# A planner that keeps TensorE's excursions to small products apart, in a GLA + RWKV-7 macaron block

## The chip, the cores and the metric

The kernel runs on one core of a Trainium2 chip. The metric is device time in microseconds of one execution. One execution in the hardware profiler gives the trace that is read here.

## The reference, cut to what matters

One layer on a sequence of 1024 rows of width 1024, all in float32:

```
x = x + 0.5 * swiglu(rms_norm(x), ffn1)          # d_ff = 2816
p = rms_norm(x) @ w_in                           # 3344 columns
o = [ GLA mixer(p) , RWKV-7 mixer(p) ]           # 512 + 512 columns, both recurrent in time
x = x + o @ w_out
x = x + 0.5 * swiglu(rms_norm(x), ffn2)
return rms_norm(x)
```

The GLA mixer keeps a 64 x 128 state for each of 4 heads. The RWKV-7 mixer keeps a 64 x 64 state for each of 8 heads; a state is multiplied by a decay, takes a rank-one correction from itself and a rank-one input at every row. Both are computed by chunks of rows, so that most of the work is small matrix products, and the chunks of one head follow one another.

## The kernel before, in words

**Halves.** The sequence is cut into two halves of 512 rows, A and B. Weights and activations of the large products are each split into a high part and a rest of type fp32r, and one large product is three matmuls (high x high, high x rest, rest x high), each 128 x 128 by 128 x 512. In this text these are the *plain products*. The mixers' products are plain float32 with tiles of 32 to 128 rows and columns: the *small products*.

**Order of the stages.** FFN 1 of A; the joint part of FFN 1 for both halves (a Strassen-like scheme, `joint_up` and `joint_down`); then for A: norm, projections (`proj`), mixers, output projection (`outproj`); then the same for B. While the mixers of A run, the ten remaining hidden blocks of B's FFN 1 are computed (generator `f1b`), and while the mixers of B run those of A's FFN 2 (`f2a`). The end is the joint part of FFN 2 and the final norm.

**The mixers (`mixers`, line 1226).** The mixers of a half are four generators, "streams", which issue a step's instructions and then yield a latency in ns or a tag to wait for:

- `loop`: RWKV's recurrence, four units u of two chunks each. A chunk has three steps: `pz`, then `pu`, then `px` and `py` together. Each needs what VectorE (DVE) or ScalarE (ACT) made of the one before.
- `prep`: for each unit, `pg` (Gram matrices), an inversion of 16 x 16 blocks in 15 rounds on VectorE (lines 106 to 108, no TensorE work) up to a transposition (line 115), then `p1`, `p1b`, `p2`, `p2b`, `pav`. Unit u may start when `loop` is through with unit u-2.
- `norm`: for each unit after `loop` is through with it, a group norm on VectorE and ScalarE (lines 226 to 233), transposes `pyT`, eight ScalarE instructions (line 244), two additions and a store.
- `both_gl`: the GLA mixer for two pairs of heads: `pkv`, `pA`, five times `pB`, `po`, two times `pt`.

**The planner** (lines 1265 to 1283) writes TensorE's order out by hand (`manual_schedule` for that engine). It keeps a clock of its own, `T.ns`, which each matmul moves on by a cost (class `PE`, line 34; 216.3 ns for a plain product). A step that was made sets its stream's due time to `T.ns` plus the latency times `SLACK` (1.49). When a stream is due, every free stream due within `NEAR` (254 ns) makes one step; then as many plain products follow as the excursion's time times `FILL` (0.3) holds, at least one; when none is due, one plain product. An *excursion* is a run of small products between plain ones. The plain products come from the filler (`f1b` or `f2a`), one matmul at each call, and end at the marker `AFTER` (hidden block 8 of 10, line 364): 480 in a half. From then on `filling` is false, and steps are written down when they come due, with nothing between.

What the planner does not fix is left to the framework, which orders the other engines, and TensorE outside of the planned part, by priority and by its own estimate of readiness. So the 96 plain products that come next in the program (`pdn` of blocks 6 and 7, then `pgu` of block 9) are laid between the last planned steps. After the last `pyT` come its ScalarE and VectorE work, a store to DRAM, the loads of the mixed rows (`outprep`, line 1285) and the output projection's first product (`pout`).

Of the kernel before, what the change touches and what calls it, by code (L numbers as in the profile page):

```python
# [372 lines left out]
BUFS = dict(s2=7, W=4, WA=2, WN=4, AR=2, UV=2, AV=2, R64=2, s1=2, i2=3, g1=3, s3=2)  # L373
SLACK = 1.490
FILL = 0.3
PAHEAD = 2
NEAR = 254.150
NH, NL, NR = 6, 6, 4
# [14 lines left out]
def block_kernel(tc, ctx, x, consts, coff, vecs, finaln, wgu, wdn, win_t, win_v, w_out, alw, wa2, g2, out):  # L393
    nc = tc.nc
    V, S, T, GP = nc.vector, nc.scalar, PE(nc.tensor), nc.gpsimd
# [67 lines left out]
    def mm3(ps, l, r, start, stop):  # L463
        T.matmul(ps, l[0], r[0], start=start, stop=False)
        T.matmul(ps, l[0], r[1], start=False, stop=False)
        T.matmul(ps, l[1], r[0], start=False, stop=stop)
# [231 lines left out]
    def stage_f(f):  # L698

        H = wk.tile([P, VW], F32R, tag="wH", bufs=NH, name="wH")[:, :HT]  # L700
        L = wk.tile([P, VW], F32R, tag="wL", bufs=NL, name="wL")[:, :HT]
        halved(f, H, L)
        return H, L
# [51 lines left out]
    def hid_dram(w, j, op):  # L755
        return dram(f"hid{w}_{j}_{op}", [P, 2 * HT])
# [92 lines left out]
    def joint_down(w, c1, c2, ep, hold, between, first=None, early=False):  # L849


        d1, d2 = slice(0, HT), slice(HT, D)
        n = len(PAIRS)
        kept = {}

        def right(i, j):

            if j not in kept:
                t = hold(j)
                for k, f in enumerate(PAIRS[j]):  # L860
                    nc.sync.dma_start(t[:, 2 * k:2 * k + 2].rearrange("p c d->p (c d)"), wdn[w][P * f:P * f + P, :])
                kept[j] = [t[:, k] for k in range(4)]
            lo0, hi0, lo1, hi1 = kept[j]
            if i in (1, 2, 3):
                return stage_f({1: lo0, 2: lo1, 3: hi1}[i])
            t = EG[:, 4 + next(turn) % 3]
            if i == 5:
                GP.tensor_tensor(t, hi0, lo0, op=SUB)
            else:
                GP.tensor_tensor(t, hi1, hi0, op=SUB)  # L870
                if i != 7:
                    GP.tensor_tensor(t, t, lo0, op=ADD)
                if i == 4:
                    GP.tensor_tensor(t, t, lo1, op=SUB)
            return stage_f(t)

        def banks(k):
            return [(pa if 4 * k + t < 5 else pm).tile([P, HT], F32, tag="pa" if 4 * k + t < 5 else "pm", name="pjd") for t in range(4)]

        def sums():  # L880
            return ep.tile([P, 7, HT], F32, tag="EG", name="EG")

        turn = iter(range(1000))
        EG = sums() if early else None
        for i in ORDER:
            ps = banks(int(i in (6, 7, 4)))
            for j in range(n):
                u = right(i, j)
                hh = first(j) if first and i == 1 else ep.tile([P, 2, HT], F32R, tag="hh", bufs=6, name="hh")
                nc.sync.dma_start(hh.bitcast(F32).rearrange("p a t->p (a t)"), hid_dram(w, j, i))  # L890
                for t in range(4):
                    to = slice(P * t, P * t + P)
                    mm3(ps[t], (hh[:, 0, to], hh[:, 1, to]), u, j == 0, j == n - 1)
            EG = EG or sums()
            E = [EG[:, t] for t in range(4)]
            for t in range(4):
                def add(x, v, k=0.5):
                    V.scalar_tensor_tensor(x, v, k, x, op0=MULT, op1=ADD)  # L898

                if i > 1:  # L900
                    x1 = c1.x[t]
                if i not in (1, 6):
                    x2 = c2.x[t]
                if i == 1:
                    S.copy(E[t], ps[t])
                    if t == 3:
                        between[1](E[t][:, 0:1])
                elif i == 6:
                    add(x1[:, d1], E[t])
                    V.tensor_tensor(E[t], ps[t], E[t], op=ADD)  # L910
                    if t == 3:
                        between[6](E[t][:, 0:1])
                elif i == 2:
                    add(x1[:, d1], ps[t])
                    add(x1[:, d2], E[t])
                elif i == 7:
                    V.tensor_tensor(E[t], ps[t], E[t], op=ADD)
                    if t == 3:
                        for y, e in zip(c2.x, E):
                            add(y[:, d1], e)  # L920
                            add(y[:, d2], e)
                        if i in between:
                            between[i](E[t][:, 0:1])
                elif i == 5:
                    add(x2[:, d2], ps[t])
                    add(x1[:, d2], ps[t])
                    if t == 3 and i in between:
                        between[i](x1[:, 0:1])
                elif i == 4:
                    add(x2[:, d1], ps[t], -0.5)  # L930
                else:
                    add(x1[:, d2], ps[t])
# [16 lines left out]
    def proj(h):  # L949
# [19 lines left out]
        def weights(ti):  # L969
            return [stage(win_t[2 * ti + kh]) for kh in range(2)]  # L970

        def product(nm):
            ps = pm.tile([P, HT], F32, tag="pm", name="pp")
            ti = TTILES.index(nm)
            us = staged.pop(ti, None) or weights(ti)
            for i in range(ti + 1, min(ti + 1 + PAHEAD, len(TTILES))):
                if ti > 1 and i not in staged:
# [248 lines left out]
    def mixers(h, filler, last):  # L1226
        hf = h.i
        d = lambda nm, cols=HT: dram(f"{nm}_{hf}", [P, cols])

        def wide(nm, cols=HT):  # L1230
            return dram(f"{nm}_{hf}", [P, 4 * cols]).rearrange("p (q t)->p q t", q=4)

        quad = Quad(g, {n: wide(n) for n in ("bv", "g", "vt", "wn0", "wn1", "mix")} |
                    {"BK": wide("BK", 2 * HT), "AR": wide("AR", 2 * HT).rearrange("p q (x t)->p q x t", x=2)})

        def gl(p):
            return gla_unit(g, p, {n: d(f"{'la' if n == 'cum' else 'kk' if n == 'k' else n}{p}") for n in ("q", "k", "cum", "qx", "kN")},
                            dram(f"vn_{hf}", [HT, HT])[:, 256 * p:256 * p + 256],
                            [d(f"go{2 * p + j}") for j in range(2)], [d(f"mix{2 * p + j}") for j in range(2)])

        tags = set()

        class Stream:
            def __init__(self, gen):
                self.gen, self.at, self.wait, self.done = gen, T.ns, None, False

            def step(self):
                try:
                    lat = next(self.gen)
                    while isinstance(lat, str) and lat[0] != "?":  # L1250
                        tags.add(lat)
                        lat = next(self.gen)
                    self.wait, lat = (lat[1:], 0.0) if isinstance(lat, str) else (None, lat)
                    self.at = T.ns + lat * SLACK
                except StopIteration:
                    self.done = True

            def free(self):
                return self.wait is None or self.wait in tags

        def both_gl():
            for p in range(2):
                yield from gl(p)

        todo = [Stream(x) for x in (quad.loop(), quad.prep(), quad.norm(), both_gl())]
        filling = True
        with tc.manual_schedule(engines={mybir.EngineType.PE}):
            while True:
                todo = [s for s in todo if not s.done]
                if not todo:  # L1270
                    break
                can = [s for s in todo if s.free()]
                t0, n = T.ns, 1
                if any(s.at <= t0 for s in can):
                    for s in can:
                        if s.at <= T.ns + NEAR:
                            s.step()
                    n = int((T.ns - t0) * FILL / 216.0 + 0.999)
                for _ in range(n):
                    if filling and next(filler, last) == last:  # L1280
                        filling = False
                if not filling and not any(s.at <= T.ns for s in can):
                    T.ns = min(s.at for s in can)
# [119 lines left out]
    def first(j):  # L1403
        if j < 4 and j % 2 == 0:
            front[j] = B.pool.tile([P, 4, HT], F32R, tag=XN[j // 2], name="hhf")
        return front[j // 2 * 2][:, 2 * (j % 2):2 * (j % 2) + 2] if j < 4 else ep.tile([P, 2, HT], F32R, tag="hh", bufs=6, name="hh")
# [147 lines left out]
```

## Time and profile before

| | us |
|---|---|
| median of 3 runs | 2138.57 |
| lowest, highest | 2127.97, 2830.62 |
| the profiled execution, its own time | 2131.11 |
| its span in the trace | 2129.3 |

The span reaches from the first to the last instruction; the other 1.8 us of that execution lie around it. The profiled execution is 0.35% below the median. The run of 2830.62 us stands apart from the two others. The trace gives each instruction's start, duration, engine, source line and tiles, who released it where it waited, and the granted clock of TensorE as a share of 2.4 GHz.

### The profile page before, as it was taken

The page shows a single profiled execution, that of the slowest core. Times are in us where ns is not written, and L with a number is a line of the kernel's source. Part 1 is how long each engine was busy: PE and PEld are TensorE (multiplying, and loading weights), DVE is VectorE, ACT ScalarE, POOL GpSimd, SP SyncE. Part 2 cuts the span into 40 slices and gives each one's busy share as a digit, 9 for nine tenths or more (in the row PEclk, how much of TensorE's full clock was granted, in tenths as well). Part 3 has the DMA queues.
Part 4 walks back from the last instruction along what each step waited for, and adds up shares of the span by engine and source line. Part 5 has one row for each costly group of instructions (what it writes and reads, how often), then busy time and mean ns, then how long its engine had stood idle before and what let it go on. Part 6 is the DMA issues. An engine that isn't in the chain of part 4 may idle for free.

```text
span 2129.3 us, 36214 instructions
## 1 busy us (share of the span) xinstructions
PE 2044.5 (96%) x13516; PEld 1633.4 (77%) x13516; DVE 1454.7 (68%) x3043; ACT 909.3 (43%) x1699; POOL 551.4 (26%) x558
## 2 busy tenths in 40 slices
PE   8999999989999999999999999999998999998998
PEld 7777888868788877767878887777776788886886
DVE  6675788747738867765476957866587577864675
ACT  6432333422446644543375644633343243432143
POOL 0411446475211300000001220000221245647610
PEclk9999999999999999999999999999998999999999
DMA  5433344587446764323435583432633334449652
GB/s 194 128 115 105 128 149 158 189 322 277 141 144 215 232 203 137 107 89 121 145 129 187 193 263 105 145 100 85 208 129 109 109 120 157 156 160 350 235 171 74
DMA packets 172639, 345.20 MB, mean 162 GB/s; under 512 B 17296, under 2 KB 56240, under 8 KB 172464
## 3 DMA queue, kind: packets, MB, share of 16 engines
q1 hardware_dynamic: 145312, 251.13, 36.1%
q0 software_dynamic: 23552, 80.76, 10.4%
q10 hardware_dynamic: 3600, 11.01, 1.5%
q8 instruction: 106, 1.74, 0.3%
q14 instruction: 69, 0.57, 0.1%
HBM read 243.21 MB, written 99.61 MB: 161 GB/s over the span
## 4 chain that ended last, share of the span: by engine, by line
PE 81%; DVE 7%; DMA 6%; ACT 3%; issue 2%; POOL 1%; SPq 0%; ACTq 0%; DVEq 0%
PE pju L43 21%; PE pgu L43 16%; PE pp L43 12%; PE pdn L43 10%; PE pjd L43 6%; PE pout L43 4%; PE pv L43 2%; PE py L43 2%; DMA hh<-d_hid 1%; PE po L43 1%; DVE x L898 1%; DVE wL L460 1%; DVE T L696 1%; DMA xw<-d_xf 1%; PE pt L46 1%
## 5 line engine op out<-in xcount | busy, mean ns | idle before, releaser
L460 DVE TENSOR_TENSOR wL<-raw,wH 128x512 fp32r<-128x512 f32 (+1 forms) x382 | 273.4, 724 | 259.9 <-ACT wH L459 259.4
L459 ACT CAST wH<-raw 128x512 fp32r<-128x512 f32 (+1 forms) x382 | 234.1, 618 | 392.6 <-PE pgu L43 126.1
L43 PE MATMUL pgu<-xnH,wH 128*128 128x512 f32 (+1 forms) x656 | 259.1, 396 | 0.3 <-ACT xnH L518 0.2
L43 PE MATMUL pgu<-xnH,wL 128*128 128x512 f32 (+1 forms) x656 | 257.9, 394 | 0.2 <-DVE wL L460 0.2
L43 PE MATMUL pgu<-xnL,wH 128*128 128x512 f32 (+1 forms) x656 | 257.8, 394 | 0.2 <-DVE xnL L519 0.2
L43 PE MATMUL pju<-T,wH 128*128 128x512 f32 x768 | 240.7, 394 | 2.4 <-ACT wH L695 2.4
L43 PE MATMUL pjd<-wH,hh 128*128 128x512 f32 x640 | 208.9, 407 | 15.0 <-DMA hh<-d_hid 14.5
L43 PEld LDWEIGHTS pju<-T,wH 128*128 128x128 f32 x768 | 144.3, 188 | 36.7 <-ACT wH L695 3.3
L43 PEld LDWEIGHTS pjd<-wH,hh 128*128 128x128 f32 x640 | 125.0, 195 | 47.3 <-issue 16.8
L43 PE MATMUL pju<-T,wL 128*128 128x512 f32 x384 | 151.4, 394 | 0.0
L43 PEld LDWEIGHTS pgu<-xnH,wH 128*128 128x128 f32 x656 | 123.8, 189 | 28.0 <-ACT xnH L518 1.0
L43 PEld LDWEIGHTS pgu<-xnH,wL 128*128 128x128 f32 x656 | 123.7, 189 | 27.9 <-issue 0.7
L43 PEld LDWEIGHTS pgu<-xnL,wH 128*128 128x128 f32 x656 | 123.8, 189 | 27.1 <-DVE xnL L519 1.0
L43 PE MATMUL pdn<-wH,hH 128*128 128x512 f32 x320 | 132.2, 414 | 11.3 <-DVE hf L668 7.7
L43 PE MATMUL pp<-xnH,wH 128*128 128x512 f32 x352 | 140.7, 400 | 0.0
L43 PE MATMUL pp<-xnL,wH 128*128 128x512 f32 x352 | 138.9, 395 | 0.0
L43 PE MATMUL pp<-xnH,wL 128*128 128x512 f32 x352 | 138.9, 395 | 0.0
L43 PE MATMUL pjd<-wL,hh 128*128 128x512 f32 x320 | 130.3, 407 | 5.8 <-DVE wL L696 5.8
L43 PE MATMUL pdn<-wH,hL 128*128 128x512 f32 x320 | 131.5, 411 | 1.2 <-DVE hL L672 1.2
L43 PE MATMUL pdn<-wL,hH 128*128 128x512 f32 x320 | 130.4, 408 | 0.9 <-DVE wL L460 0.9
L631 DVE SCALAR_TENSOR_TENSOR x<-pdn,x 128x512 f32<-128x512 f32 x144 | 98.7, 687 | 33.0 <-PE pdn L43 31.8
L696 DVE TENSOR_TENSOR wL<-s,wH 128x512 fp32r<-128x512 f32 x96 | 99.1, 1034 | 29.7 <-ACT wH L695 29.6
(393 smaller groups left out, 4317.5 us busy)
## 6 DMA issues: line engine op xcount, KB each, us to landing
raw<-in_wgu_dram SPq DMA_DIRECT2D x256, 256.0 KB, 2.7
hh<-d_hid SPq DMA_DIRECT2D x80, 512.0 KB, 4.4
d_hid<-hh POOLq DMA_DIRECT2D x76, 512.0 KB, 3.7
raw<-in_win_t_dram SPq DMA_DIRECT2D x88, 256.0 KB, 3.2
raw<-in_wdn_dram SPq DMA_DIRECT2D x80, 256.0 KB, 2.7
wdk<-in_wdn_dram SPq DMA_DIRECT2D x24, 512.0 KB, 7.0
d_x<-x SPq DMA_DIRECT2D x20, 512.0 KB, 2.6
raw<-in_w_out_dram SPq DMA_DIRECT2D x32, 256.0 KB, 3.0
```

The costliest lines, as they stand in the source:

```text
L43: return self.t.matmul(out,lhsT,rhs,**kw)
L46: return self.t.transpose(out,in_,idn)
L459: S.copy(H, raw)
L460: V.tensor_tensor(L, raw, H.bitcast(F32), op=SUB)
L631: V.scalar_tensor_tensor(h.x[tt][:, co], ps, 0.5, h.x[tt][:, co], op0=MULT, op1=ADD)
L696: V.tensor_tensor(L, f, H.bitcast(F32), op=SUB)
L898: V.scalar_tensor_tensor(x, v, k, x, op0=MULT, op1=ADD)
```

## The change: what it does

A constant `APART` of 1700 ns is added, and the planner notes in `back` its clock at the end of the last excursion that had TensorE work. While the filler lasts, no stream makes a step before the planner's clock is at `back + APART`, even if it is due. A plain product counts 216.3 ns, so eight of them lie between two excursions (seven count 1514 ns). Streams that fall due in the meantime make their steps together afterwards. Steps without TensorE work are held back too, but do not set `back`. The first edit of the diff, in `joint_down`, drops a Python name that is not read in that pass and issues nothing.

```diff
 FILL = 0.3
+APART = 1700.0
...
-                if i not in (1, 6):
+                if i not in (1, 2, 6):
                     x2 = c2.x[t]
...
         filling = True
+        back = 0.0
...
-                if any(s.at <= t0 for s in can):
+                if any(s.at <= t0 for s in can) and (not filling or t0 >= back + APART):
                     for s in can:
                         if s.at <= T.ns + NEAR:
                             s.step()
+                    if T.ns > t0:
+                        back = T.ns
                     n = int((T.ns - t0) * FILL / 216.0 + 0.999)
```

## Rows read from the trace of the kernel before

**Rows 1.** The page: span, busy time by engine, chain that ended last.

```profile
span 2129.3 us, 36214 instructions
PE 2044.5 (96%) x13516; PEld 1633.4 (77%) x13516; DVE 1454.7 (68%) x3043; ACT 909.3 (43%) x1699; POOL 551.4 (26%) x558
PE 81%; DVE 7%; DMA 6%; ACT 3%; issue 2%; POOL 1%; SPq 0%; ACTq 0%; DVEq 0%
```

**Rows 2.** Stretches: start:end, length, busy (x instructions) by engine, clock, DMA share, GB/s.

```profile
761.30:976.60 215.30, 207.37 (x3069) 158.52 (x3068) 152.65 (x570) 102.57 (x206) 2.32 (x6) 0.98 0.41 125
976.60:1007.40 30.80, 27.44 (x166) 20.91 (x165) 19.68 (x44) 11.67 (x23) 0.00 (x0) 1.00 0.40 127
1263.10:1479.70 216.60, 207.12 (x3069) 158.64 (x3068) 152.73 (x570) 102.45 (x206) 3.58 (x7) 0.98 0.41 124
1479.70:1509.60 29.90, 27.35 (x166) 20.96 (x165) 20.86 (x44) 11.65 (x23) 5.59 (x6) 1.00 0.43 132
```

**Rows 3.** Timeline of TensorE around two excursions: start, duration, instruction, tiles.

```profile
806.14 0.50 PE L43 MATMUL pdn<-wH,hL 128*128 128x512 f32 x1
806.48 0.39 PE L43 MATMUL pdn<-wH,hH 128*128 128x512 f32 x1
806.71 0.39 PE L43 MATMUL pdn<-wL,hH 128*128 128x512 f32 x1
...
807.26 0.69 PE L43 MATMUL p2b<-R,X 32*32 32x32 f32 x32
807.89 0.73 PE L43 MATMUL pB<-qe,ar 64*32 64x16 f32 x64
808.54 0.50 PE L43 MATMUL pdn<-wH,hH 128*128 128x512 f32 x1
```

**Rows 4.** The same timeline: first excursion; one with two tile shapes; one alone.

```profile
774.39 2.06 PE L43 MATMUL pg<-AR,BK 64*128 64x128 f32 x32
...
813.42 0.68 PE L43 MATMUL pz<-X,AR 64*64 64x64 f32 x16
814.03 2.06 PE L43 MATMUL pg<-AR,BK 64*128 64x128 f32 x32
...
831.45 0.68 PE L43 MATMUL pz<-Xn,AR 64*64 64x64 f32 x16
832.07 0.50 PE L43 MATMUL pgu<-xnH,wL 128*128 128x512 f32 x1
```

**Rows 5.** TensorE's waits, 774 to 1010 us: total us, times, longest.

```profile
PE p2b L43 <- ACT X L141: 3.7, 2, 2.0
PE pout L43 <- ACT xnH L1290: 3.3, 1, 3.3
```

**Rows 6.** Stretches of 5 us with the clock, columns as in Rows 2.

```profile
915.00:920.00 5.00, 4.86 (x63) 3.67 (x65) 1.90 (x4) 2.84 (x6) 0.00 (x0) 0.66 0.33 87
...
1620.00:1625.00 5.00, 5.00 (x16) 3.96 (x16) 4.58 (x9) 2.12 (x4) 0.00 (x0) 0.68 0.01 2
```

**Rows 7.** Timeline of TensorE: unit 3 of half A, up to the output projection.

```profile
922.75 2.06 PE L43 MATMUL pg<-AR,BK 64*128 64x128 f32 x32
...
938.64 0.69 PE L43 MATMUL px<-UV,WN 128*64 128x64 f32 x16
...
941.36 0.51 PE L43 MATMUL pgu<-xnH,wH 128*128 128x512 f32 x1
...
949.71 0.75 PE L43 MATMUL p<-D,c 32*32 32x32 f32 x64
...
982.36 0.34 PE L43 MATMUL py<-UV,W 128*64 128x64 f32 x4
...
993.65 0.63 PE L46 MATMUL pyT<-ct,AV 128*128 128x128 f32 x4
...
1007.40 0.50 PE L43 MATMUL pout<-wH,xnH 128*128 128x512 f32 x1 [3.34 <-ACT xnH L1290]
```

**Rows 8.** Timeline of VectorE: the transposition that ends unit 3's inversion.

```profile
947.85 0.44 DVE L115 STREAM_TRANSPOSE D<-R 128x256 f32<-128x256 f32 x1
```

## The prediction, on record before the result

> **What bounds the kernel now.** I read the page first, then the two mixer stretches cut where the filler ends, then TensorE's timeline, its waits, and the clock. The page shows TensorE at 96% of the span and 81% of the chain that ended last [rows 1]: time is saved only by shortening TensorE's own work or its waits. The change touches TensorE's order alone, and that only between 761 and 1007 us (half A) and between 1263 and 1510 us (half B). Each stretch has a first part, which lasts until the filler's 480 plain products are used up (215.3 and 216.6 us), and a tail from there to the first product of the output projection (30.8 and 29.9 us) [rows 2]. The reader should see that the halves are alike within 1.3 us, so I work out half A and double it; half A is 246.1 us.
>
> In the first part TensorE is busy 207.4 of 215.3 us [rows 2]. The waits with names are two of `p2b` on a ScalarE copy, 3.7 us together; in the tail `pout` waits 3.3 us [rows 5]. So there is little idle time to win, and the question is what an excursion costs and who pays for the delay.
>
> **An excursion's price.** Plain products follow each other at 0.23 us (806.48 to 806.71). Four of them between two excursions take 1.12 us (806.14 to 807.26), which is 0.19 more than 4 x 0.2325: a longer step in and another out [rows 3]. Two small steps in one excursion keep their own times: `p2b` takes 0.63 to the `pB` behind it, `pB` 0.65 to the plain product [rows 3]; `pz` takes 0.61 to a `pg` of another tile shape and 0.62 to a plain product [rows 4]. So joining two excursions saves 0.19 us. The Trainium skill, in "TensorEngine Tiling (Array Packing)", Key Properties, says that a change of tiling mode drains TensorE, whoever follows; by that rule joined steps of different shapes would save nothing, and the saving below of 3.4 us a half would be near 0. The trace disagrees, by the 0.61 beside 0.62.
>
> **The new order.** The loop can be stepped through with its own constants: costs, latencies x 1.49, 0.3, 254, and now 1700. For the loop as it stands this gives the order in the trace, from the `pg` at 774.39 [rows 4] to the `pyT` at 993.65 [rows 7]: 59 excursions, 56 of them before the filler ends, at which point only `pu`, `px`/`py` and `pyT` of the last chunk are left. With the new gate it gives 38 excursions before the filler ends, nearly all eight plain products apart. But the chain of the recurrence is stretched: where 5 or 7 products stood between its steps there are now 8. The 480 products are used up while `px`/`py` of unit 2, second chunk, are due. Still to come are all of unit 3 (`p1`, `p1b`, `p2`, `p2b`, `pav`, two chunks) and the `pyT` of units 2 and 3. It is an order, not a time; the times below are the trace's.
>
> **First part, half A.**
> - Small products that move behind the filler's end: three `px`/`py` at 2.72 (938.64 to 941.36 [rows 7]) = 8.2; four `pz`/`pu` at 0.61 = 2.4; four 32 x 32 steps at 0.63 = 2.5; `pav` with twice `pz`'s matmuls, 1.2 by estimate; two `pyT` at 0.4 (estimate from its 0.63 in the row, which overlaps the next) = 0.8. Together 15.1, of which 3.7 were there before: -11.4.
> - Switches: (56 - 38) x 0.19 = -3.4.
> - The `p2b` waits: with 8 instead of 5 products ahead of it, and `pyT`'s eight ScalarE instructions started one excursion earlier, unit 2's wait goes; unit 3's moves into the tail: -3.7. After such a wait the clock reads 0.66 over 5 us [rows 6], so 3.4 us at 1.2 instead of 2.4 GHz, a loss of 1.7; two of these: -3.4. Late next is nothing on TensorE: the products stand 8 deep.
> - The dropped name in `joint_down` issues nothing: 0. Steps held back without TensorE work (the inversion's rounds) cost nothing here, as VectorE takes them when ready; what they delay is in the order already.
>
> 215.3 - 11.4 - 3.4 - 3.7 - 3.4 = 193.4 us.
>
> **Tail, half A.** 96 plain products remain to cover it, 96 x 0.2325 = 22.3 us, with 15.1 of small ones and some ten switches (1.9): 39.3 us of work, as a floor. Against it stands a chain:
> 1. Unit 3's inversion. From the end of `pg` (922.75 + 1.99) to the end of the transposition is 23.5 us [rows 7, 8]. In the new order `pg` ends 30 plain products, three switches, one `px`/`py` and two `pz`/`pu` ahead of the filler's end: 7.0 + 0.6 + 2.7 + 1.2 = 11.5. So `p1` can start 12 us into the tail. If VectorE has less else to do it is sooner; I bound it by 8 and 12.
> 2. `p1` to the last `py`: 11.6 us of small products (four 0.63, `pav` 1.2, two chunks of 3.94) and seven hand-overs to ScalarE or VectorE. None shows free of cover. Behind seven products (1.8 us) none stalls, and three products (0.9) already hide one; I take 1.0 each, 7.0, between 6.3 and 12.6. `pyT` of unit 2 stands between `p1` and `p1b`, so its ScalarE instructions meet `p2b`'s copies again: 2.0 [rows 5], between 0 and 4. Sum 20.6.
> 3. Last `py` to `pyT`: 982.63 to 993.65, 11.0 us [rows 7], with the evacuations of `pdn` on the same VectorE. These come earlier now; I take 9.5, between 7 and 11.
> 4. `pyT` to `pout`: 993.65 to 1007.40, 13.75 us [rows 7]: ScalarE, a store, loads behind it. Nothing shortens it.
>
> 12 + 20.6 + 9.5 + 13.75 = 55.9 us, against 39.3 of work: some 16 us idle where 3.3 were. The idle time falls mostly between the last `pyT` and `pout`, since the 96 products go into the first gaps. The clock falls there as it does now; a stretch that resumes after a longer idle time reads 0.68 over 5 us, about the 0.66 after a 2 us wait [rows 6], so a long wait costs no more than a short one.
>
> **Sum.** 193.4 + 55.9 = 249.3 against 246.1: +3.2 us a half, +6.4 in all. 2131.11 + 6.4 = **2137.5 us**, 2138 rounded. This is against the profiled execution, which lies 0.35% under the median 2138.57; two undisturbed runs 10.6 us apart say how much a run can stray.
>
> **Rivals.**
> - *The tail is covered better, the change gains.* At the lower bounds the chain is 8 + 11.6 + 6.3 + 7 + 13.75 = 46.7 us, a half 240.1, -6 each: **2119**. It decides where the chain falls below 246.1 - 193.4 = 52.7. For it: VectorE is 71% busy in the first part [rows 2] and need not hold up the inversion as long as in the row. Against it: every link was measured with the same engines at the same work.
> - *The tail is longer.* Upper bounds: 12 + 11.6 + 12.6 + 4 + 11 + 13.75 = 65, plus two slow clocks of 1.7: 68.4, a half 261.8, +15.7 each: **2162**. The mechanism is one: `pyT` in front of `p1b` in TensorE's fixed order makes unit 3 wait for unit 2's group norm on a VectorE that is also inverting. For it: the very collision shows already [rows 5]. Slower by 2% needs a tail of 74 us.
> - *The order does nothing.* If the framework's placing fills the tail with products from behind the output projection, the idle time only moves there; with the saved switches and waits that is **2120 to 2131**. Against it: in the trace `pout` waited 3.3 us [rows 5], and nothing was put into that gap.
>
> **How the numbers follow.** Chances: forecast 0.5 (2126 to 2149), gain 0.23, longer tail 0.2, order without effect 0.07. The range that leaves out 2 in 10 reaches from the gain to the longer tail, widened a little below for an undisturbed run: 2112 to 2162. A change of under 2% (43 us) can't be told from none in runs of this kernel; faster by that would need 21 us a half, more than all its savings and `pout`'s wait together (3.4 + 3.7 + 3.4 + 3.3 = 13.8), slower a tail of 74 us. So faster 0.02, within 0.94, slower 0.04.
>
> **What would show it.** Right: eight plain products between most excursions; 38 before the filler ends; the first part near 193 us; a tail near 56 us with `pout` waiting 10 us or more; no `p2b` wait on ScalarE for unit 2. Wrong: a `pout` wait still near 3 us (the tail was covered), first part much over 193 us (joined steps wait for PSUM or each other, or switches inside an excursion cost as much as outside), or plain products of blocks 8 and 9's `pdn` ahead of `pout`.

## The result, and the profile after

The changed kernel takes 2154.26 us (median of 4 runs, 2152.24 to 2156.82). The kernel before, run beside it, took 2127.97, 2130.12 and 2138.57 us; single runs that stand far apart (2830.62 us of before, 2292.02 us of `slack_only` below) are left out of the medians and ratios given here. The ratio is 1.0105, 95% interval 1.0083 to 1.0127: slower by some 22 us, where 6.4 were forecast. The profiled execution of after took 2156.82 us, its span is 2155.0, 25.7 us longer than before's.

The page of after: span, busy time by engine, and the instruction queue of TensorE (for later).

```profile
span 2155.0 us, 36208 instructions
PE 2042.8 (95%) x13516; PEld 1632.9 (76%) x13516; DVE 1460.6 (68%) x3043; ACT 910.2 (42%) x1699; POOL 548.1 (25%) x558
...
q8 instruction: 106, 1.74, 0.3%
```

Against [rows 1] TensorE has the same 13516 products and 1.7 us less busy time. So its idle time grew by 27.4 us, and that is where the longer span comes from. The stretches, first part and tail of half A, then of half B, columns as in [rows 2]:

```profile
759.38:960.77 201.39, 194.40 (x2746) 150.35 (x2744) 143.98 (x535) 93.42 (x185) 2.33 (x6) 0.98 0.44 131
960.77:1012.85 52.08, 38.24 (x489) 28.37 (x487) 28.90 (x80) 21.59 (x45) 0.00 (x0) 0.89 0.27 83
1269.69:1475.74 206.05, 195.96 (x2746) 151.68 (x2744) 145.04 (x535) 93.19 (x185) 3.56 (x7) 0.98 0.42 127
1475.74:1534.48 58.74, 38.48 (x489) 28.30 (x488) 34.24 (x80) 21.61 (x45) 13.35 (x15) 0.85 0.34 112
```

Half A is 253.5 us (before 246.1), half B 264.8 (before 246.5): +7.4 and +18.3, together the 25.7; what lies before, between and behind the halves cancels within 0.1 us. The first parts became 13.9 and 10.6 us shorter, the tails 21.3 and 28.8 longer. In the tails TensorE works 38 us and is idle 13.8 and 20.3.

TensorE's timeline in the first part of A, where [rows 3] had four plain products between excursions (start, duration, instruction, idle before it):

```profile
800.31 0.75 PE L43 MATMUL p<-D,c 32*32 32x32 f32 x64
800.99 0.73 PE L43 MATMUL pB<-qe,ar 64*32 64x16 f32 x64
801.65 0.50 PE L43 MATMUL pdn<-wH,hH 128*128 128x512 f32 x1
...
803.36 0.40 PE L43 MATMUL pdn<-wL,hH 128*128 128x512 f32 x1
803.69 0.36 PE L43 MATMUL p1b<-R,X 32*32 32x16 f32 x20
804.60 0.55 PE L43 MATMUL p1b<-R,X 32*32 32x16 f32 x44 [0.55 <-issue]
```

Two steps in one excursion, eight plain products, the next. `p` takes 0.68 to the `pB` behind it: joined steps keep their own times, as forecast. The last row is a wait inside a step; it becomes important.

TensorE's waits in half A (756 to 1013 us), which answer to [rows 5]: total us, times, longest. `pout` and the longest of the `pyT` waits lie in the tail:

```profile
PE pout L43 <- ACT xnH L1294: 9.7, 1, 9.7
PE pyT L46 <- DVE AV L233: 4.8, 3, 3.7
PE pA L43 <- DVE ke L289: 2.1, 2, 1.6
PE pgu L43 <- issue: 1.1, 1, 1.1
PE pg L43 <- DVE oN L345: 0.9, 1, 0.9
PE p L43 <- DVE nwt L493: 0.6, 1, 0.6
PE p1b L43 <- issue: 0.6, 1, 0.6
```

and half B:

```profile
PE pout L43 <- ACT xnH L1294: 11.2, 1, 11.2
PE pyT L46 <- DVE AV L233: 8.6, 3, 7.4
PE pB L43 <- issue: 4.2, 4, 1.3
PE pA L43 <- DVE ke L289: 3.1, 2, 2.6
```

The 3.7 us of `p2b` are gone (0.2 is left), and others stand in their place: the first part of A idles 7.0 us where it idled 7.9. Beside those of `p2b`, before had these waits there:

```profile
PE pA L43 <- DVE ke L289: 1.8, 2, 1.3
PE pkv L43 <- DMA kN<-d_kN: 1.3, 1, 1.3
PE pB L43 <- issue: 0.6, 1, 0.6
```

New in the first parts of after are waits for VectorE at `pyT` (1.1 us in A, 1.2 in B), at `pg` (0.9 in each) and at `p` on `nwt` (0.6 and 0.4). The waits without a named releaser (`issue`) grew to 1.8 us in A and 4.2 in B. After a wait the clock falls as it did [rows 6]: 5 us of half B behind the last of the four `pB`:

```profile
1385.00:1390.00 5.00, 3.73 (x75) 2.97 (x72) 2.92 (x7) 1.36 (x3) 0.00 (x0) 0.72 0.16 50
```

The tail of A, answering to [rows 7]; the filler ends at 960.77:

```profile
967.59 0.75 PE L43 MATMUL p<-D,c 32*32 32x32 f32 x64
...
972.24 0.63 PE L46 MATMUL pyT<-ct,AV 128*128 128x128 f32 x4
972.79 0.73 PE L43 MATMUL p1b<-R,X 32*32 32x16 f32 x64
...
992.88 0.34 PE L43 MATMUL py<-UV,W 128*64 128x64 f32 x4
1002.02 1.09 PE L46 MATMUL pyT<-ct,AV 128*128 128x128 f32 x4 [3.70 <-DVE AV L233]
1012.85 0.80 PE L43 MATMUL pout<-wH,xnH 128*128 128x512 f32 x1 [9.74 <-ACT xnH L1294]
```

The chain is the forecast one: `p1` 6.8 us into the tail, `pyT` of unit 2 ahead of `p1b`, last `py`, `pyT`, `pout`.

### The profile page after: what moved, and what is told of

Read it like the earlier page. It is cut to its first block, busy times and chain, and to the rows that moved or that the text cites. A ratio compares the mean times of both kernels' runs of the same rounds, so it can differ in the third digit from the quotient of the medians.

```text
span 2155.0 us, 36208 instructions
## 1 busy us (share of the span) xinstructions
PE 2042.8 (95%) x13516; PEld 1632.9 (76%) x13516; DVE 1460.6 (68%) x3043; ACT 910.2 (42%) x1699; POOL 548.1 (25%) x558
## 3 DMA queue, kind: packets, MB, share of 16 engines
q0 software_dynamic: 23552, 80.76, 10.4%
q8 instruction: 106, 1.74, 0.3%
## 5 line engine op out<-in xcount | busy, mean ns | idle before, releaser
L43 PE MATMUL pjd<-wH,hh 128*128 128x512 f32 x640 | 209.3, 407 | 12.9 <-DMA hh<-d_hid 12.5
L697 DVE TENSOR_TENSOR wL<-s,wH 128x512 fp32r<-128x512 f32 x96 | 102.2, 1066 | 28.8 <-ACT wH L696 28.7
```

Of the source, the lines that this page charges most:

```text
L43: return self.t.matmul(out,lhsT,rhs,**kw)
L697: V.tensor_tensor(L, f, H.bitcast(F32), op=SUB)
```

## Experiments

Sizes below are of the profiled execution, A and B in this order: first part, tail.

### The gate's size, and joining without a gate

```diff
# gate_1000: after          # gate_2000: after          # near_800: before
-APART = 1700.0             -APART = 1700.0             -NEAR = 254.150
+APART = 1000.0             +APART = 2000.0             +NEAR = 800.0
```

> APART 1000 instead of 1700: five plain products at least. The planner's loop then gives 51 excursions before the filler ends (54 to 56 without the gate, 39 with 1700), and what is left after it is only the last unit's pu, px/py, pz, pu, px/py and pyT. Theory Tail: tail about 34 us against 30.8, first part 4 to 5 us shorter, so the total is within 6 us of the kernel before, 2125 to 2137. Theory Joined: the loss goes with the number of joined excursions, 3 to 5 of 16, so 4 to 7 us of the 20 to 24, 2136 to 2140. They come close here; the lengths of first part and tail tell them apart.

> APART 2000: ten plain products. The planner's loop gives 33 excursions before the filler ends, but most of unit 2 and all of unit 3 are then left (with 1700: unit 3). Theory Tail: first part 20 to 25 us shorter than before, tail about 70 us instead of 52 to 58, so another 8 to 15 us a half over the 1700 kernel, 2165 to 2185. Theory Joined: six fewer excursions than with 1700 on top of sixteen, so 6 to 9 us more, with the tail's waits as they are, 2158 to 2164; or, if joining pays its 0.19 us and the 1700 kernel lost only by chance of its order, no more than 2154.

> The kernel before, without the gate, with NEAR 800 instead of 254 ns: streams due within the next 0.8 us make their step in the same excursion. So excursions are joined by taking steps early, not by holding them back: 50 excursions, and at the filler's end only the last pyT is left, so the chain runs ahead of where it stood before. Theory Tail: tail shorter (22 to 26 us against 30.8), first part longer by what moved into it (some 4 us), pout's wait of 3.3 us gone or below 2: 2120 to 2131, not slower than before. Theory Joined: the joined excursions cost as in the changed kernel, so 2135 or more.

`gate_1000`: 2131.55 us, ratio to before 0.9998 [0.9985, 1.0011]; 205.4 and 208.8, tails 40.0 and 39.1. `gate_2000`: 2151.79 us, 1.0089 [1.0062, 1.0116]; 183.1 and 183.3, tails 69.2 and 75.4. `near_800`, which joins steps more readily but holds none back: 2134.05 us, 1.0003 [0.9986, 1.0020]; 219.8 and 227.0, tails 25.6 and 26.0. `gate_1000` came out in Tail's range, with tails longer than its 34 us. `near_800` lies between the two theories: its tails are Tail's, its first parts 4.5 and 10.4 us longer than before's.

The widest gate has the fewest excursions (33 before the filler ends; 39 in after, 54 in before) and the shortest first parts, with 3 us idle in each. So joined excursions don't cost: 2151.79 us is below that theory's 2158, and in line with the case put beside it, that joining pays and 1700 lost by its order. What the gate takes from the first part it adds to the tail. Tail's price for 2000 was too high, since the first part's waits went as well.

### The tail: more cover, and the chain

```diff
# tail_dn3: after
-    run(f1b, n=3)
+    run(f1b, n=5)
...
-    run(f2a, n=3)
+    run(f2a, n=5)
# pyt_p3: after, in norm()
+            if u==2: yield "?P3"
# gate_L0: after
-                if any(s.at <= t0 for s in can) and (not filling or t0 >= back + APART):
+                if any(s.at <= t0 for s in can) and (not filling or "L0" in tags or t0 >= back + APART):
```

> The changed kernel, with the last down products of the filler's FFN (pdn of blocks 8 and 9, 48 plain products, 11.2 us) put in the program ahead of the output projection, in both halves. Theory Tail (the filler is used up too early in the chain, so that TensorE has nothing left while the last group norm, store and loads run): the waits of the last pyT and of pout, 3.7 + 9.7 us in half A and 7.4 + 11.2 in half B, shrink by some 8 to 11 us in each half; since the same 48 products no longer cover the first norm behind the output projection, 8 to 10 us of idle time appear there, so the sum stays within -5 to 0 us of the changed kernel, 2149 to 2155. Theory Joined (joined excursions themselves cost: fetch of instructions, drains): the tail's waits are not the loss; the first part keeps its length and the total does not move. What both would miss: a total far below 2149 would say that nothing needed those products behind the projection.

2155.38 us, 1.0108 [1.0086, 1.0131]. With 144 plain products instead of 96 the tails idle 7.6 and 15.0 us (13.8 and 20.3 in after) but are 56.5 and 67.5 us long, and behind the halves 6 us each are saved: nothing in sum. The products fill gaps, and the chain gets longer: in half B the last `py` is 15.7 us ahead of `pyT` (12.5 in after), and `pyT` to `pout` takes 14.6 and 17.9 us (10.8 and 12.3). That it is their evacuations on VectorE which do this was not tested. The tail is bound by the chain, not by a lack of work.

> The changed kernel, with unit 2's transposes pyT held until unit 3's pav is written down. In the changed kernel TensorE's fixed order has pyT of unit 2 ahead of p1b of unit 3, and p1b started 4.65 us after p1, where its own input takes under a microsecond. Theory Order (the fixed order makes unit 3 wait for unit 2's group norm): p1b starts 1 to 2 us after p1, and the tail gets 2 to 4 us shorter in each half, 2147 to 2151; some of it is lost where the eight ScalarE instructions behind pyT now meet the copies of unit 3's chunks. Rival (the tail is bound by TensorE's own work up to the last py, not by this wait, since plain products lie in between): the last py does not come earlier and the total stays within 2 us.

2144.27 us, 1.0051 [1.0034, 1.0069]: 10 us less than after, and below the expected range. With `pyT` of unit 2 held until unit 3's preparation is through, `p1b` starts 1.6 us after `p1` (5.2 in after), and the tails are 48.3 and 52.8, 4 and 6 us shorter. So the mechanism of the forecast's second rival, `pyT` ahead of `p1b`, is real. Only half A gives its price, 4 us: in half B the group norm now ended before GpSimd's additions began (1511.7 us), so that the collision of the next section was absent too.

> The changed kernel, with the gate of 1700 ns only until unit 0 of the recurrence is through. The planner's loop then gives 48 excursions before the filler ends, and the same steps left after it as with APART 1000 (two chunks of unit 3 and pyT). Theory Tail: tail 38 to 41 us as with APART 1000 (40.0 and 39.1), not 52 to 59, first part shorter than before by about 10 us; total like the kernel before, 2124 to 2134, although the first third of the mixers is joined exactly as in the changed kernel. Theory Joined: that third holds 8 of the 16 joined excursions, most of them, so about half the loss stays, 2140 to 2145.

2149.58 us, 1.0087 [1.0060, 1.0115], with runs from 2141.9 to 2156.0; the profiled one, at the low end, shows 210.5 and 213.0, tails 40.5 and 40.2. The tails are Tail's, but the total lies outside what either theory gave. Why the runs differ by 14 us is left open.

### Half B: GpSimd beside VectorE

VectorE in the last group norm of after's half B, and GpSimd at that time:

```profile
1515.63 0.16 DVE L494 TENSOR_TENSOR nwt<-nwt,nwa 128x8 f32<-128x8 f32 x1
...
1516.31 1.22 DVE L495 SCALAR_TENSOR_TENSOR nwy<-nwt,nwy 128x8 f32<-128x8 f32 x1
...
1518.24 2.85 DVE L494 TENSOR_TENSOR nwt<-nwt,nwa 128x8 f32<-128x8 f32 x1
```

```profile
1515.85 1.66 POOL L718 TENSOR_TENSOR xs<-xnH,xnL 128x512 f32<-128x512 f32 x1 [35.29 <-DVE nwt L494]
...
1518.57 2.49 POOL L718 TENSOR_TENSOR xs<-xnH,xnL 128x512 f32<-128x512 f32 x2
```

The operation that takes 0.16 us alone took 2.85 and ended at 1521.09, as the additions did (1521.06); the one of 1.22 ended at 1517.53, the addition at 1517.51. The Trainium skill, in "SBUF — State Buffer", Who interferes with whom, says that a VectorE instruction with two SBUF inputs contends with a GpSimd instruction that reads SBUF, over ports that are an exclusive lock. These rows agree; the longer operation lasted over two additions. `pyT` waits 7.4 us there, in half A 3.7.

```diff
# store_later: after             # store_gated: store_later, and in to_store()
-    to_store(A)                 +            V.tensor_copy(t[:, 0:1], gate)
     outproj(B)                               GP.tensor_tensor(t, ...)
+    to_store(A)                 +    to_store(A, B.x[0][:, 0:1])
```

> The changed kernel, with the store of A's normed rows (to_store, GpSimd additions of 128x512 and their DMAs) put behind B's output projection in the program. In the changed kernel two small VectorE instructions of B's last group norm took 1.22 and 2.85 us instead of 0.17 and ended with GpSimd instructions that ran beside them; that is 3.7 of the 7.4 us which the last pyT waits in half B. Theory GpSimd (these additions hold VectorE up): pyT's wait in half B falls to about 3.7 us as in half A, B's tail from 58.7 to 53 to 55 us, half A stays, the total falls by 3 to 6 us, 2148 to 2152. Theory Chain only (VectorE would be late anyway, by other work): nothing moves by more than 1.5 us.

2153.89 us, 1.0089 [1.0068, 1.0111], and inconclusive: the framework laid the additions at the same time as before (1512 to 1521), and the two instructions took 1.23 and 2.85 us again.

> As after, but the eight additions of half A's stream to its store (on GpSimd) can't begin before the first addition of half B's output projection has ended: a one-column copy of its result goes into each tile first. Theory Beside: in half B the last group norm's two small VectorE instructions took 1.22 and 2.85 us because GpSimd's additions ran beside them, and that is why pyT waited 7.4 us there against 3.7 in half A. Then they take 0.2 us each, pyT waits 3 to 4.5 us, B's tail falls from 58.7 to 54 to 56 us, and the kernel takes 2149 to 2152 us. Rival Own Order: VectorE reaches that group norm late by its own work (the evacuations of pdn between), whatever GpSimd does: pyT still waits over 6 us, the tail stays at 58 us or more, and the time is 2153 to 2158 us.

2151.65 us, 1.0098 [1.0078, 1.0119]. The additions start at 1559, the group norm's instructions are short:

```profile
1517.83 0.16 DVE L494 TENSOR_TENSOR nwt<-nwt,nwa 128x8 f32<-128x8 f32 x1
...
1518.51 0.16 DVE L495 SCALAR_TENSOR_TENSOR nwy<-nwt,nwy 128x8 f32<-128x8 f32 x1
...
1519.40 0.17 DVE L494 TENSOR_TENSOR nwt<-nwt,nwa 128x8 f32<-128x8 f32 x1
```

`pyT` waits 3.73 us and the tail is 53.3 us: theory Beside holds, at 5.4 us of half B's tail. The total does not show it: the interval overlaps that of after, and this execution's first part of B is 209.7.

### The waits without a releaser

In half B of after four `pB` wait for nothing that the trace names, 4.2 us in all. Each stops in the middle of a step:

```profile
1380.29 0.53 PE L43 MATMUL pB<-qe,ar 64*32 64x16 f32 x40
1382.00 0.38 PE L43 MATMUL pB<-qe,ar 64*32 64x16 f32 x24 [1.19 <-issue]
...
1384.98 0.71 PE L43 MATMUL pB<-qe,ar 64*32 64x16 f32 x63
1386.97 0.17 PE L43 MATMUL pB<-qe,ar 64*32 64x16 f32 x1 [1.27 <-issue]
```

Numbering all of TensorE's instructions in the trace from 0 (loads, products and the 281 of its sequencer, which wait for semaphores), these are numbers 17090, 18625, 18882 and 19137: remainders 194, 193, 194, 193 of 256. In the twenty profiles of this case, the mixers of both halves have 86 unnamed waits of over 0.15 us; 82 stand at these two remainders, whatever the product and the order. The other four are at a `pkv`.

The page's instruction queue q8 moved 1.74 MB in 106 packets, 16.4 KB each, and TensorE's 27313 instructions are 106 times 256 and 177 more. In the four versions below that add 128 or 256 instructions it moved 107. The Trainium skill, in "Runtime: NRT & Kernel Launch", Instruction fetch mechanics, says that instructions arrive in blocks of 256 and that this is mostly hidden. The remainders agree with the block; the waits of up to 2.5 us (in `slack_only`, below) do not agree with the hiding.

The trace names no releaser for these waits, but it has the start and end of each packet, and these settle what they wait for:

| run, step | wait, us | packet ended | step went on | between |
|---|---|---|---|---|
| after, `pB` | 1.19 | 1380.79 | 1382.00 | 1.21 |
| after, `pB` | 1.27 | 1385.55 | 1386.97 | 1.42 |
| `slack_only`, `pB` | 2.53 | 795.83 | 797.30 | 1.47 |

The packets pair off with the blocks in order: the wait that ends at 1382.00 stands at instruction 18882, 73 times 256 and 194 more, and the packet that ended at 1380.79 is the 73rd. All 82 waits end 1.15 to 1.60 us after their block's packet, and in none of the profiles does any block begin less than 1.12 us after its own. So TensorE stops for its own instructions. 256 instructions of plain products last near 30 us (128 x 0.2325 [rows 3]); where the waits of after stand, 256 went by in 3.5 to 5.3, the wait included. A short block alone makes no wait: `shift_one`, below, has blocks of 3.3 to 4.6 us without one. Why a packet comes early or late is open.

Both versions issue the first `pB` of half A again, into the same place, with the planner's clock left as it was. It is work that the kernel does not need.

```diff
# shift_128 as here; shift_one has range(2 ...)
-                    T.matmul(pB[h][...],...)
+                    for again in range(3 if li==0 and not hasattr(g,"moved") else 1):
+                        T.t.matmul(pB[h][...],...)
+                    T.ns+=63
+        g.moved=1
```

> As after, but the first pB of half A is issued three times instead of once (the same 32 products into the same place), which adds 128 instructions of TensorE (64 loads, 64 products) ahead of everything behind it, without altering the order written out. Theory Block: TensorE's unnamed waits inside runs of small products lie at every 256th instruction, because instructions come in blocks of 256 and a run of small products uses a block up in under 5 us. Then the waits at pB of half B (1320, 1377, 1382 and 1387 us in after, 4.2 us together) leave their products and stand 128 instructions earlier or later in the program, at the same remainder of the count; their sum in half B is anything from 0 to 5 us, and the total 2150 to 2157 us. Rival Hazard: these products wait for their PSUM tiles or for each other: the waits stay at the same four products with the same 4.2 us, and the total rises by 1.3 us, the length of the added products.

2159.20 us, 1.0139 [1.0126, 1.0153]. The expectation miscounts: one `pB` is 64 products and 64 loads, so two more are 256 instructions, a whole block. Two of the waits stayed in the same `pB` (after 40 and 63 products again), as either theory has it then; the total is 2 us above the range given.

> As after, but the first pB of half A is issued twice: one pB is 64 products and 64 loads, so 128 instructions of TensorE more ahead of all that follows, half a block of 256. (Issued three times it added 256, a whole block, and the unnamed waits stayed at the same four products of half B, which tells nothing apart.) Theory Block: they leave the pB that are stopped after 48, 40 and 63 of their 64 products in after (at 1377.3, 1382.0 and 1387.0 us) and any unnamed wait stands 128 instructions from the old places, still at remainder 193 or 194 of the count of TensorE's instructions; half B's sum of them lies between 0 and 5 us, the kernel takes 2149 to 2158 us. Rival Hazard: the same pB wait after the same number of their products, 4.2 us together, and the time is that of after plus 0.65 us.

2147.72 us, 1.0082 [1.0057, 1.0107]. The same two `pB` and the first parts of A and B:

```profile
1376.14 0.73 PE L324 MATMUL pB<-qe,ar 64*32 64x16 f32 x64
...
1380.01 0.73 PE L324 MATMUL pB<-qe,ar 64*32 64x16 f32 x64
```

```profile
760.26:958.07 197.81, 191.97 (x2810) 149.19 (x2809) 144.12 (x535) 93.22 (x185) 2.32 (x6) 1.00 0.44 133
...
1269.60:1468.00 198.40, 192.91 (x2746) 149.71 (x2745) 144.55 (x535) 93.29 (x185) 3.56 (x7) 0.99 0.45 133
```

In half B no `pB` is interrupted; one unnamed wait of 0.20 us is left there, in a `p1b` at instruction 17089, remainder 193, and one of 0.44 us in half A. Hazard is refuted, and the total is just below Block's range. With 0.65 us of work more the first parts are 3.6 and 7.6 us shorter: the unnamed waits went, and with them slow clock (mean 0.98 in after, 1.00 and 0.99 here). Part of the 7.6 is chance: the waits of `pA` on VectorE are 1.3 us shorter in this execution, and slow clock followed one of them in after. The gain is seen again, though. Four more profiles with the old remainder have 200.2 to 205.0 us in A and 203.0 to 209.7 in B (`store_later`, `store_gated`, `tail_dn3`, `shift_128`); `shift_gated`, below, has 198.7 in both. The intervals of the totals overlap. Before was not run with the shift, so how much of its own time is such luck is open.

### Gate and stretch

`slack_only` is the kernel before with another constant, the others are after:

```diff
-SLACK = 1.490
+SLACK = 1.300   # slack_only, slack_130, s130_a1350, s130_a1700
+SLACK = 1.400   # slack_140
+SLACK = 1.000   # s100_a1700
-APART = 1700.0
+APART = 1000.0  # slack_130, slack_140
+APART = 1350.0  # s130_a1350
```

> APART 1000 and SLACK 1.3 instead of 1.49: the gate keeps five products between excursions, but a step is due sooner, so that the chain is not stretched. The planner's loop gives 48 excursions and only the last pyT left after the filler's end. Theory Tail: tail 24 to 27 us as with NEAR 800 (25.6 and 26.0). The open side is the first part: steps that come sooner wait more (with NEAR 800 idle 10.9 and 13.7 us, against 5.8 and 7.8 with APART 1000). If they wait no more than with APART 1000, the total is 2118 to 2126, below the kernel before; if they wait as with NEAR 800, 2130 to 2136.

> The kernel before with latencies stretched by 1.3 instead of 1.49 and no gate: the control of the version with both 1.3 and a gate of 1000, which took 2127.5 us. Theory Gate: the fewer switches of a gate of 1000 are worth 1 to 2 us a half, so without it the time is 2129 to 2134 us, as the kernel before. Theory Stretch: the shorter stretch alone gives it, as the tail's wait at pout goes (3.3 and 2.5 us in before): 2125 to 2129 us, with pout waiting under 1 us, and 55 or more excursions before the filler ends.

> After with the gate at 1000 instead of 1700 and latencies stretched by 1.4 instead of 1.49, between two versions: 1.49 gave first parts of 205 and 209 us and tails of 40 and 39 us; 1.3 gave 223 and 223, and 23 and 24 us. Theory Tail (what a shorter first part saves beyond the tail's wait is lost in the tail, and the other way round): in the middle pout waits 1 to 3 us and the first part idles 8 to 10, so a half is 243 to 246 us and the kernel takes 2122 to 2129 us. Rival Flat: what leaves pout's wait turns into waits of the first part one for one, a half stays 246 to 248 us and the kernel 2129 to 2134 us.

> After with a stretch of 1.3 and a gate of 1350, between the 1000 that took 2127.5 us and 1700. Theory Sum: first parts of 212 to 220 us, tails of 26 to 36 us with pout waiting 0 to 5 us, halves of 243 to 250 us, the kernel 2122 to 2135 us. Theory Gate: with 1.49 a gate of 1000 had tails of 40 us, so one of 1350 has them at 44 to 48 whatever the stretch: halves of 250 to 254 us, the kernel 2138 to 2148 us.

> After, with latencies stretched by 1.3 instead of 1.49; the gate stays at 1700. Theory Sum: gate and stretch both delay the chain of the recurrence, and the tail grows with what they add up to. A shorter stretch takes some 3 to 6 us of each chain of dependent steps back: tails of 40 to 48 us, first parts of 205 to 210 us, the kernel 2134 to 2148 us, faster than after. Theory Gate: the eight products between excursions set the order alone, and the stretch counts for nothing behind them: 39 excursions again, tails of 52 to 59 us, the kernel 2149 to 2157 us.

> After without any stretch of the latencies (1.0), the gate at 1700 alone. Theory Sum: the chain is delayed by the gate only: tails of 30 to 42 us; steps now come due before their operands are there, and eight products hide part of that, so first parts of 210 to 225 us with 8 to 16 us idle: the kernel 2125 to 2150 us. Theory Gate: tails of 50 us or more as with 1.49, and the waits of the first part on top: 2155 to 2180 us.

| stretch, gate | us | ratio to before [95%] | first parts | tails |
|---|---|---|---|---|
| 1.3, none | 2163.21 | 1.0145 [1.0108, 1.0182] | 248.4, 245.1 | 22.8, 22.8 |
| 1.3, 1000 | 2127.54 | 0.9976 [0.9961, 0.9992] | 223.3, 223.1 | 22.9, 23.9 |
| 1.4, 1000 | 2136.55 | 1.0032 [1.0018, 1.0045] | 223.5, 225.8 | 25.3, 25.8 |
| 1.3, 1350 | 2136.94 | 1.0025 [1.0010, 1.0039] | 209.3, 211.5 | 39.6, 40.9 |
| 1.3, 1700 | 2150.97 | 1.0088 [1.0068, 1.0108] | 204.2, 206.7 | 48.0, 51.8 |
| 1.0, 1700 | 2139.49 | 1.0041 [1.0027, 1.0054] | 210.8, 215.5 | 36.1, 36.3 |

The control missed both its theories: without a gate a stretch of 1.3 costs 1.45%, some 31 us. TensorE's longest waits of its half A, and that first part:

```profile
PE p2b L43 <- ACT X L141: 4.2, 2, 2.2
PE pyT L46 <- DVE AV L233: 4.2, 2, 3.8
...
PE pB L43 <- issue: 2.8, 2, 2.5
```

```profile
756.64:1005.03 248.39, 225.80 (x3133) 170.79 (x3132) 159.89 (x591) 101.26 (x207) 2.31 (x6) 0.90 0.38 110
```

The steps come before their operands; 22 us of waits and a mean clock of 0.90 (0.98 in before) follow. The first part of half A of `slack_130`, with the gate of 1000 on top:

```profile
757.37:980.71 223.34, 210.58 (x3133) 162.31 (x3132) 157.50 (x585) 101.31 (x207) 2.31 (x6) 0.96 0.41 121
```

So a gate of 1000 is worth 25 and 22 us of first part where steps come too early. At 2127.54 us that version lies between the two ranges of its expectation, and is 0.24% faster than before. Stretch and gate buy the same thing, time between dependent steps, and pay with the same coin, the tail: at 1700 the tail falls from 52 to 48 to 36 us in half A as the stretch goes from 1.49 to 1.3 to 1.0. That settles for Sum against Gate at 1.0; at 1.3 the tails lie between the two and the total is in Gate's range. In none of these orders is there a free middle: 1.4 with 1000 (2136.55 us, above both ranges given) and 1.3 with 1350 (2136.94, between the two) are slower than 1.3 with 1000.

### Both causes together, and a faster version

```diff
# shift_gated: shift_one with the edits of store_gated
# s130_shift: shift_one with
+SLACK = 1.300
+APART = 1000.0
```

> After with both: the first pB issued twice, which moves TensorE's count by 128, and half A's additions to its store held until half B's output projection has its first sum. Theory Two Causes (these two make up the miss): half A as with the one pB more, 249.9 us; half B 198.4 + 53 to 54, 251 to 253 us; the kernel 2140 to 2144 us. Rival Not Additive: what half B gains in the tail is lost to new waits at other 256th instructions or at pout: half B 255 to 258 us, the kernel 2146 to 2151 us.

2141.98 us, 1.0056 [1.0035, 1.0077], as Two Causes had it. First part and tail of A, then of B:

```profile
759.86:958.53 198.67, 193.77 (x2809) 150.52 (x2808) 143.97 (x535) 93.13 (x185) 2.32 (x6) 0.99 0.45 132
958.53:1010.41 51.88, 37.73 (x489) 28.07 (x487) 28.92 (x80) 21.59 (x45) 0.00 (x0) 0.91 0.28 86
1267.77:1466.43 198.66, 192.96 (x2746) 149.77 (x2744) 143.91 (x535) 93.28 (x185) 2.32 (x6) 0.99 0.44 132
1466.43:1519.58 53.15, 37.79 (x490) 28.08 (x488) 28.95 (x80) 21.63 (x46) 0.00 (x0) 0.90 0.28 83
```

Halves of 250.6 and 251.8 us: alike again, and 1.3 and 2.5 above the forecast 249.3.

> The version with latencies stretched by 1.3 and a gate of 1000 (2127.5 us), with the first pB of half A issued twice. There the unnamed waits took 2.4 us in half A and 1.3 us in half B, at remainder 193 or 194 of the count. Theory Block: a shift by half a block moves them; at the new places five blocks pass in 2.9 to 4.0 us, three in half A and two in half B against two and two now, so the shift is a throw of dice here: first parts 219 to 226 us, the kernel 2122 to 2132 us. Rival Dense: waits stay at the same pB and only the 0.65 us is added: 2128 to 2129 us, first parts as they were.

2125.11 us, 0.9974 [0.9962, 0.9986]: faster than both kernels, than before by some 6 us (0.26%). First parts 222.3 and 220.7, tails 22.9 and 23.9. It was not run against 2127.54 side by side, so whether the shift adds anything there is not shown; of the unnamed waits 0.4 and 1.0 us are left, where 2.4 and 1.3 stood.

## Why the prediction was wrong, by its own steps

- **The order.** Right but for one excursion: 39 before the filler ends, not 38. For before it had 56, where the trace has 54. So 15 switches fell away and not 18, 2.9 us and not 3.4. The planner's clock is not at zero when the mixers start, so the first excursion is not held back, and the filler ends behind unit 2's last `px`/`py`, not ahead of it. That moves one `px`/`py` and its switch, 2.72 + 0.19 = 2.9 us, from the tail to the first part: 196.3 and 53.0 are the forecasts to compare.
- **An excursion's price.** Right: joined steps of different shapes keep 0.68 and 0.66 us. With the most joining (`gate_2000`) nothing is lost in the first part.
- **The step that failed: "the `p2b` waits: -3.7 ... two of these: -3.4. Late next is nothing on TensorE".** The `p2b` waits went, but idle time in the first part stayed: 7.0 and 10.1 us for 7.9 and 9.5 before. So did the slow clock: TensorE had 1.2 GHz for 6.8 and 10.2 us of the first parts, for 10.2 in each before, which gives back 1.7 us in A and nothing in B. First parts came out at 201.4 and 206.0 for 196.3 (in B 197.6, since before's is longer there). Of these 5.1 and 8.4 us, idle time is 2.8 and 4.3, the clock 1.7 and 3.4, the switches 0.5 each.
- **What was late next.** Two things that no step of the sum had. One is VectorE: `pyT`, `pg` and `p` on `nwt`, which never waited in before's first parts, wait 2.6 and 2.4 us. The other is TensorE's own instructions: the unnamed waits rose from 0.6 to 1.8 us in A and from 1.6 to 4.2 in B, and the clock fell behind some of them. Before had such waits too (0.55 us in A, 1.26 and 0.36 in B), so the signs were in the trace; the prediction left them in the 4.2 us of other waits and let these stand unchanged. `shift_one` shows what the second is worth: 128 instructions more ahead, the same order, and the first parts are 197.8 and 198.4. It is not shown that joined steps bring such waits: `gate_2000` joins most and has 0.3 us of them in each half. Where they fall depends on the count, so this part of the miss is bad luck.
- **"The halves are alike within 1.3 us, so I work out half A and double it"** failed with it. The tail of B is 58.7 us, not 52.1: 5.4 of these are GpSimd's additions beside VectorE's last group norm, as `store_gated` shows. In before that norm lay at 1493 to 1496 us, where GpSimd made none.
- **The tail of half A**: 52.1 for 53.0, though its links were off both ways: `p1` at 6.8 us (forecast 12 less 2.9), `p1` to the last `py` 25.6 for 20.6, then 8.8 for 9.5, then 10.8 for 13.75. `pyT` of unit 2 ahead of `p1b`, priced at 2.0, is worth 4 us by `pyt_p3`. "Nothing shortens it", said of `pyT` to `pout`, was wrong by 3 us. That the sum of the tail is so close is luck.
- **The sum.** With both causes taken away 2142 us is measured for 2138 forecast: of the miss of 16 us the two were worth 12, by the ratios to before (1.0105 and 1.0056) 10. The shift does not do away with the first cause; it moves it to where it costs little. Of the rest the halves hold 3.8 us: first parts of 198.7 for 196.3, 4.7 in all, less 1.0 in the tails.
- **The other cases.** The gain did not come: the tail could not be covered better even with more products (`tail_dn3`). The longer tail's mechanism was there (`pyt_p3`), but tails of 52.1 and 58.7 us are far from its 68.4. And the order was not without effect.

## What to carry over

Holding steps apart in a fixed order and stretching their latencies are one lever: each buys waits out of the stretch with filler and lengthens what is left when the filler ends, so a gate is worth trying where waits are many (25 us of half A's first part at a stretch of 1.3) and costs where they are gone already. When two stages look alike, look at what other engines do beside each before doubling a sum. When one wait is taken away, look for what is late next behind it, on every engine that the step needs. And look at where unnamed waits stand in an engine's instruction count before leaving them out of the sum: if they come at a fixed remainder, any edit upstream moves them, and some us of a result are luck.

## What the runs showed of the hardware

- Runs of small products on TensorE (or the first plain product behind one) stop for 0.2 to 2.5 us at one place in 256 instructions (remainder 193 or 194 of the count of all its instructions, 82 of 86 unnamed waits), where 256 were used up within 3.0 to 6.3 us. The stop ends 1.15 to 1.60 us after a 16 KB packet of the instruction queue. Moving the count by 128 took the first parts from 201.4 and 206.0 us to 197.8 and 198.4, with the same order of work; the kernel went from 2154.26 to 2147.72 us (each against its own runs of before: 1.0105 and 1.0082, intervals that overlap).
- A 128x8 VectorE operation on two tiles, 0.16 us alone, took 2.85 us beside GpSimd's 128x512 additions, to within 0.03 us of their end.
